# Hybrid decoder block on one core: bias parts split on ACT and DVE inside the merge, an eleventh weight tile in flight, the first gather done block by block

## Chip, cores and metric

One core of a Trainium2 chip runs the whole program. The metric is the device time of one execution in microseconds (us): median of 3 runs of the kernel before 1238.84 us (1238.54 to 1238.99). All data are float32; DMA is moved by 16 engines, and the weights of 32 experts (384 MiB) pass through the core once.

## The reference, cut to what matters

```python
h = rms_norm(x, g_norm_mix) * (1 + scale1) + shift1        # x is 256 tokens x 1024
z = h @ w_in                                               # four mixers' inputs and the merge logits
ys = ...                                                   # MoBA, GLA, retention, sliding window
up = einsum('bsnc,ncd->bsnd', ys, w_branch)
mixed = sum(sigmoid(merge_logits) * up, over the 4 branches) @ w_out
x = x + gate1 * mixed
h2 = rms_norm(x, g_norm_ffn) * (1 + scale2) + shift2
combine = softmax over the top 4 of (h2 @ w_router + b_router)   # 32 experts
for e in range(32):
    gu = h2 @ w_gate_up[e] + b_gate_up[e]                  # 1024 x 2048 weights
    act = min(glu, 7) * sigmoid(1.702 * min(glu, 7)) * (clip(lin, -7, 7) + 1)
    y += combine[:, e] * (act @ w_down[e] + b_down[e])     # 1024 x 1024 weights
out = rms_norm(x + gate2 * y, g_final)
```

## The kernel before

**Front.** Everything up to the router is one pass over the input weights. Each weight block is split into a rounded part and a remainder (function `split`, L347 on ACT writes the part `wh`, L348 on DVE the remainder `wl`), and TensorE multiplies both. The merge is the last piece of it: four branches (`for bi, n in enumerate(order)`), four units of 256 columns in each, numbered `at` 0 to 15 here. A unit makes 48 products for the merge logits (`pz_m`, L361), a sigmoid on ACT (`msg`, L816), 12 products for the branch (`pu`, L823), and on DVE `msg<-pu,msg` (L830) and the addition into `mix` (L831). In units 1 to 11 the conditioning rows are worked off beside it: accumulations `acs` on DVE (L243, L245), and in the odd units eight transposes `pmt` (L267). Units 12 to 15 also multiply by the output weights (`pw`).

**Bias parts.** The gate and up bias of the experts (32 x 2048) is added by TensorE from three bfloat16 parts whose sum is the float32 bias. They are made once: the bias is loaded three times below each other into `bgu` (L791, DMAs of the ACT queue), and GpSimd (POOL) casts, subtracts and casts again (L794, L798, L799) into `bias_sb`. The code stands at the beginning of branch 2, but a scheduler of the language orders each engine's instructions by data and by a cost of its own, so they run earlier, in units 5 to 7.

**Expert stream.** An expert's weights are six tiles of 2048 KB (`wg` x4 for gate and up, `wd` x2 for down). SP issues the loads in order, each into one of ten slots of a cyclic list (`seq`: five of `ring`, three of `rx`, one each of `hp` and `r9`), and a load waits until the products that read the slot's last tile are done. The first ten tiles (`units`: all of experts 0 and 1 but the last two of expert 1) are loaded ahead, while the merge ends and the router runs.

**Router and first gather.** `x1_logits` and the loop over `t` make the top-4 masks and the position of each token in its expert's list. `n2h` and `n2l` hold the normalised rows, split like the weights (ACT L924, L955 and DVE L927). `gather_first` then forms `he`, the 64 rows of each of the first four experts: `pm` (0/1 matrices, L1006), 32 gather products `pg` (L1019, 8 to a block of 256 channels), and a scale and shift of each block on DVE (L1030) and ACT (L1027). After a block the function `first` may use it: `gate_up_part` (L1124) multiplies two rows of 128 channels with one `wg` tile. All of `n2l` was made before the first block, and the gather products of all blocks had been put ahead of the first gate and up products. `combine` (the routing weights) and `pwt`, `psm` (L1075, L1090) follow; then experts run in pairs.

Of the kernel before, what the change touches and what calls it, by code (L numbers as in the profile page):

```python
# [20 lines left out]
P = 128  # L21
S = 256
NT = S // P
# [19 lines left out]
def hybrid_block_kernel(ctx, tc, x, c, w_ada, b_ada, g_norm_mix, w_in, w_gla_gate, b_gla_gate, g_gla_norm,  # L43
# [5 lines left out]
    def f32(ap):  # L49
        return ap.bitcast(F32)  # L50
# [313 lines left out]
    def z_unit(tiles, c0, name, token, sw=False):  # L364
        pz = bank("z", f"pz_{name}")
        for i in range(2):
            wh, wl = split(tiles[i][:, :, c0:c0 + 256], 4, 256, f"{name}_{i}", sw)
            for j in range(2):
                z_part(pz, wh[:, 2 * j:2 * j + 2, :], wl[:, 2 * j:2 * j + 2, :], 2 * i + j, token)
                bg()  # L370
                slow_step()
        return pz
# [407 lines left out]
    for bi, n in enumerate(order):  # L780
        if bi == 2:
            finish()
            mixers.close()
            add_slots(ctx.enter_context(tc.tile_pool(name="rx", bufs=EXTRA)), EXTRA)
            lb = ctx.enter_context(tc.tile_pool(name="lb", bufs=1))
            bias_sb = lb.tile([P, D], F32, tag="bias", name="bias_sb")
            bgu, bdn = bias_sb.bitcast(BF16), bias_sb[3 * NE:, :]
            sel = lb.tile([P, NE], BF16, tag="sel", name="sel")
            bt = wtile("bgu32")
            for g in range(3):  # L790
                A.dma_start(bt[NE * g:NE * g + NE, :], b_gate_up[0])  # L791
                V.tensor_copy(sel[NE * g:NE * g + NE, :], ident[NE * g:NE * g + NE, NE * g:NE * g + NE])
            A.dma_start(bdn, b_down[0])
            G.tensor_copy(bgu[0:3 * NE, :], bt[0:3 * NE, :])  # L794
            for g0 in (1, 2):
                for g in range(g0, 3):
                    r = slice(NE * g, NE * g + NE)
                    G.tensor_tensor(bt[r, :], bt[r, :], bgu[r, :], ALU.subtract)  # L798
                    G.tensor_copy(bgu[r, :], bt[r, :])  # L799
        wb = wtile(f"wb{n}").rearrange("p (k f) -> p k f", f=1024)  # L800
        nc.sync.dma_start(wb, w_branch[0, n].rearrange("(k p) f -> p k f", p=P))
        yh, yl = ysp[n]
        for u in range(4):
# [8 lines left out]
            if at == 12:  # L812
                router_weights()
            pz = z_unit(wz, (u % 2) * 256, f"m{n}_{u}", False)
            sg = mp.tile([P, 512], F32, tag="t2", name=f"msg{n}_{u}")
            A.activation(sg, pz, AF.Sigmoid)  # L816
# [38 lines left out]
    scr = cp.tile([P, NT, D], F32, tag="xn", name="scr")  # L855
    ssq2 = cp.tile([P, NT, 4], F32, tag="ssq2", name="ssq2")
    pls = [bank("z", f"pl{t}") for t in range(NT)]
    sq_i, pl_i = {}, {}
# [9 lines left out]
    def x1_logits(t, g):  # L868
# [7 lines left out]
        if g == 1 and t == 1:  # L876
            A.activation(xt[:, 0:2], pt4[:, 0:2], AF.Copy)
            V.tensor_copy(xt[:, 2:4], pt4[:, 2:4])
        else:
            A.activation(xt, pt4, AF.Copy)  # L880
# [6 lines left out]
    for k in (KC - 2, KC - 1):  # L887
        out_split(k, 0)
    units = [wg_src(e, j) for e in range(2) for j in range(4)] + [wd_src(0, j) for j in range(2)]
    half.clear()  # L890
# [21 lines left out]
    n0 = first_n2.enter_context(tc.tile_pool(name="n0", bufs=1, side="right"))  # L912
    n2h = n0.tile([P, NT, D], F32R, tag="hi", name="n2h")
    n2l = n0.tile([P, NT, D], F32R, tag="lo", name="n2l")
    comb = epa.tile([P, NT, NE], F32, tag="comb", name="comb")
# [4 lines left out]

    def n2_first(t):
        cs = slice(0, 256)
        with tc.issue_after(sq_i[NT - 1, 1]):
            A.activation(n2h[:, t, cs], x_sb[:, t, cs], AF.Copy, scale=rss[t])  # L924

    def n2_low(t, cs):
        return V.scalar_tensor_tensor(n2l[:, t, cs], x_sb[:, t, cs], rss[t], f32(n2h[:, t, cs]), ALU.mult,  # L927
                                      ALU.subtract).ins

    with tc.issue_after(pl_i[1]):  # L930
        gate_rows(5, "ab")
    for t in range(NT):
# [3 lines left out]
        rss.append(ssq2[:, t, 3:4])  # L936
        n2_first(t)
        V.scalar_tensor_tensor(lg[:, t, :], pls[t][:, 0:NE], rss[t], brt, ALU.mult, ALU.add)
# [9 lines left out]
    with tc.issue_after(mask_i):  # L948
        n2_low(0, slice(0, 256))
    V.scalar_tensor_tensor(pos, pp[:, 0:NT * NE].rearrange("p (t e) -> p t e", t=NT), 1.0, mask, ALU.add, ALU.mult)  # L950
    for q in range(1, 4):
        for t in range(NT):
            cs = slice(q * 256, (q + 1) * 256)
            with tc.issue_after(sq_i[NT - 1, 1]):
                A.activation(n2h[:, t, cs], x_sb[:, t, cs], AF.Copy, scale=rss[t])  # L955

# [25 lines left out]


    last_i = {}

# [47 lines left out]
    def gather_first(then):  # L1033
        pm, he = one_hot(0)
        with tc.issue_after(last_i["pm"]):
            n2_low(1, slice(0, 256))
        for q in range(1, 4):
            with tc.issue_after(last_i["pm"]):
                for t in range(NT):
                    n2_low(t, slice(q * 256, (q + 1) * 256))  # L1040
        for k2 in range(KC // 2):
            cs = slice(k2 * 256, (k2 + 1) * 256)
            gather_part(0, k2, pm, he, n2h[:, :, cs], n2l[:, :, cs])
            then(k2, he)
        return he, pm
# [442 lines left out]
```

## Time and profile before

| | |
|---|---|
| median of 3 runs | 1238.84 us |
| profiled execution: time / span | 1239.36 us / 1237.6 us |
| busy PE / DVE / ACT / POOL | 1137.6 / 499.1 / 236.0 / 41.6 us |
| moved by DMA | 470.40 MB, mean 380 GB/s |
| mean granted TensorE clock | 0.979 |

The span is cut into 40 slices of 30.9 us on the page; a digit is the busy share of a slice in tenths. Durations below come from the one profiled execution, starts are us from its span's beginning. PE is TensorE, SP the engine that issues most DMAs.

### The profile page before, as it was taken

To read this page: it belongs to the slowest core of one execution; us is meant where nothing else is said; L and a number is where in the kernel's file an instruction comes from. 1 tells how busy PE (TensorE), PEld (TensorE's weight loads), DVE (VectorE), ACT (ScalarE), POOL (GpSimd) and SP (SyncE) were. 2 spreads that over 40 slices of the span, in tenths; PEclk is the share of its full clock that TensorE was granted. 3 is DMA by queue.
4 is the path that set the end of the run, shared out by engine and by line. 5 is a ranking of instruction groups with operands and counts; after the bars stand their busy time and mean duration, and the time that the engine had idled before them with its cause. 6 is when DMAs were issued, how large, how long until landed. Compare 5 with 4: busy or idle time off the path is not lost.

```text
span 1237.6 us, 14530 instructions
## 1 busy us (share of the span) xinstructions
PE 1137.6 (92%) x6134; PEld 580.3 (47%) x6134; DVE 499.1 (40%) x845; ACT 236.0 (19%) x409; POOL 41.6 (3%) x64
## 2 busy tenths in 40 slices
PE   6999986999999999999989998999999898889895
PEld 4788886998433333333333333333333333333334
DVE  3597699866322323232223223222222322232244
ACT  3466332444200200020011002001100200020000
POOL 2000107000000000000000000000000000000000
PEclk9999998999999998999999999999999999999998
DMA  9977479738799999999999999999999999999994
GB/s 320 349 276 256 153 268 347 282 155 371 308 430 426 429 427 427 428 427 429 427 428 429 426 428 427 428 426 428 427 427 429 426 427 428 428 427 428 428 423 152
DMA packets 63643, 470.40 MB, mean 380 GB/s; under 512 B 6362, under 2 KB 18771, under 8 KB 39156
## 3 DMA queue, kind: packets, MB, share of 16 engines
q1 hardware_dynamic: 62736, 467.37, 91.6%
q10 hardware_dynamic: 836, 2.04, 0.5%
q8 instruction: 50, 0.82, 0.3%
q14 instruction: 21, 0.17, 0.0%
HBM read 468.35 MB, written 1.05 MB: 379 GB/s over the span
## 4 chain that ended last, share of the span: by engine, by line
PE 72%; DMA 16%; DVE 9%; issue 1%; ACT 1%; POOL 0%; POOLq 0%; ACTq 0%; DVEq 0%; SPq 0%
PE ea L1124 15%; PE ed L1150 14%; PE eb L1124 14%; DMA wg<-in_w_gate_up_dram 9%; PE pz_m L361 6%; DMA wd<-in_w_down_dram 6%; PE pg L1019 3%; PE pw L768 2%; PE py L1167 2%; DVE wl_m L348 1%; PE pu L823 1%; PE eat L1138 1%; DVE y_sb L1172 1%; DVE nl L1055 1%; DMA wada<-in_w_ada_dram 1%
## 5 line engine op out<-in xcount | busy, mean ns | idle before, releaser
L1124 PE MATMUL ea<-wg,he 128*64 128x512 f32 x1024 | 281.3, 607 | 5.0 <-DMA wg<-in_w_gate_up_dram 5.0
L1124 PE MATMUL eb<-wg,he 128*64 128x512 f32 x1024 | 278.2, 600 | 0.0
L1150 PE MATMUL ed<-wd,aT 128*64 128x512 f32 x960 | 221.4, 606 | 6.6 <-DMA wd<-in_w_down_dram 6.6
L1124 PEld LDWEIGHTS eb<-wg,he 128*64 128x64 f32 x1024 | 78.2, 139 | 149.4 <-issue 149.4
L1124 PEld LDWEIGHTS ea<-wg,he 128*64 128x64 f32 x1024 | 73.3, 138 | 129.4 <-issue 114.5
L1150 PEld LDWEIGHTS ed<-wd,aT 128*64 128x64 f32 x960 | 67.1, 139 | 133.0 <-issue 120.5
L1100 ACT ACTIVATE es<-eg 128x512 f32<-128x512 f32 x32 | 20.2, 631 | 511.2 <-DVE eg L1098 511.2
L1098 DVE TENSOR_SCALAR eg<-ea 128x512 f32<-128x512 f32 x32 | 22.1, 692 | 235.5 <-PE ea L1124 235.5
L361 PE MATMUL pz_m<-hhl,wh_m 128*128 128x256 f32 x512 | 96.9, 289 | 0.6 <-ACT wh_m L347 0.6
L361 PE MATMUL pz_m<-hhl,wl_m 128*128 128x256 f32 x256 | 73.9, 289 | 10.7 <-DVE wl_m L348 10.7
L361 PEld LDWEIGHTS pz_m<-hhl,wh_m 128*128 128x128 f32 x512 | 81.4, 195 | 1.5 <-ACT wh_m L347 0.8
L1140 DVE COPY aT<-eat 128x512 f32<-128x512 f32 x32 | 22.1, 692 | 84.0 <-PE eat L1138 84.0
L361 PEld LDWEIGHTS pz_m<-hhl,wl_m 128*128 128x128 f32 x256 | 49.9, 195 | 11.7 <-DVE wl_m L348 11.7
L1172 DVE TENSOR_TENSOR y_sb<-y_sb,py 128x512 f32<-128x512 f32 x56 | 36.0, 684 | 37.8 <-PE py L1167 37.8
L1019 PE MATMUL pg<-pm,nl 128*128 128x256 f32 x112 | 36.7, 344 | 15.7 <-DVE nl L1055 15.4
L1019 PE MATMUL pg<-pm,nh 128*128 128x256 f32 x112 | 34.6, 316 | 17.1 <-ACT nh L1054 17.1
L1160 DVE TENSOR_TENSOR obl<-ed,obh 64x512 fp32r<-64x512 f32 x30 | 20.7, 689 | 71.7 <-ACT obh L1159 71.4
L1030 DVE TENSOR_SCALAR he<-pg,G,modT 128x256 f32<-128x256 f32 x32 | 17.2, 542 | 78.9 <-PE pg L1019 78.9
L348 DVE TENSOR_TENSOR wl_m<-win_m,wh_m 128x1024 fp32r<-128x1024 f32 x26 | 44.7, 1732 | 7.6 <-ACT wh_m L347 7.6
L1054 ACT ACTIVATE nh<-x_sb,ssq 128x256 fp32r<-128x256 f32 x56 | 25.3, 499 | 80.3 <-PE pg L1019 80.3
L347 ACT ACTIVATE wh_m<-win_m 128x1024 fp32r<-128x1024 f32 x26 | 27.5, 1059 | 66.1 <-PE pz_m L361 51.4
L1019 PEld LDWEIGHTS pg<-pm,nh 128*128 128x128 f32 x112 | 21.9, 195 | 33.1 <-ACT nh L1054 27.5
(441 smaller groups left out, 1363.9 us busy)
## 6 DMA issues: line engine op xcount, KB each, us to landing
wg<-in_w_gate_up_dram SPq DMA_DIRECT2D x128, 2048.0 KB, 27.6
wd<-in_w_down_dram SPq DMA_DIRECT2D x62, 2048.0 KB, 28.8
wada<-in_w_ada_dram SPq DMA_DIRECT2D x14, 1024.0 KB, 11.3
win_m<-in_w_in_dram SPq DMA_DIRECT2D x13, 1024.0 KB, 8.8
win_c<-in_w_in_dram SPq DMA_DIRECT2D x8, 1024.0 KB
wada<-in_w_ada_dram SPq DMA_DIRECT2D x12, 512.0 KB, 7.5
wada<-in_w_in_dram SPq DMA_DIRECT2D x3, 1024.0 KB, 10.5
wo<-in_w_out_dram SPq DMA_DIRECT2D x3, 1024.0 KB, 8.3
```

The lines of the kernel that those rows point to most:

```text
L347: A.activation(wh, src, AF.Copy)
L348: V.tensor_tensor(wl, src, f32(wh), ALU.subtract)
L361: T.matmul(pz[:, b * 256:(b + 1) * 256], l, r, start=(kh == 0 and b == 0 and kk == 0 and i == 0), stop=last and i == 2, skip_group_check=True)
L768: T.matmul(pw[t, hf_], m_[:, kk, t * P:(t + 1) * P], w[:, 0, :], start=(k == 0 and i == 0), stop=(k == KC - 1 and i == 2))
L1019: last_i["pg"] = T.matmul(pg[:, kk * 256:(kk + 1) * 256], n2[:, t, :].rearrange("p (c r) -> p r c", r=2)[:, kk, :], pm[:, t, :, 0:2], star ...
L1054: A.activation(nh[:, t, :], x_sb[:, t, cs], AF.Copy, scale=rss[t])
L1098: V.tensor_scalar(g, pa, 7.0, None, ALU.min)
L1124: last_i["gu"] = T.matmul(pp_[64 * j:64 * j + 64, :], he[:, k, (e % EB) * CAP:(e % EB + 1) * CAP], w[:, i * DE + j * 512:i * DE + (j + 1) ...
L1140: V.tensor_copy(aT, pt.rearrange("p (q s) -> p q s", q=4))
L1150: last_i["ed"] = T.matmul(pd[64 * jj:64 * jj + 64, :], aT[:, k % 4, 64 * (k // 4):64 * (k // 4) + 64], w[k % 4][:, (jj ^ sw) * 512:(jj ^ s ...
L1167: T.matmul(py, s_[:, hf_, t * P:(t + 1) * P], o_, start=(i == 0), stop=(i == 1))
L1172: V.tensor_tensor(yv, yv, py, ALU.add)
```

## The change

Three edits. (1) The bias parts are made in four column pieces of 512, by `bias_part(u)` in the four units of branch 2: ACT makes the bfloat16 copies (12, over 96, 64 and 32 partitions), DVE the two subtractions of each piece (8); POOL makes none. (2) An eleventh tile is loaded ahead. The ten slots now take three `wg` tiles of expert 0, four of expert 1 and three `wd` tiles; the fourth `wg` tile of expert 0 goes into pool `n0`, where `n2h` and `n2l` lay and where the experts' work tiles lie later. (3) `n2` is kept as four blocks of 256 channels for the high and low part, the low parts are made one block at a time, and each block's gate and up products are put behind the next block's gather.

```diff
-            G.tensor_copy(bgu[0:3 * NE, :], bt[0:3 * NE, :])
-            for g0 in (1, 2):
-                for g in range(g0, 3):
-                    r = slice(NE * g, NE * g + NE)
-                    G.tensor_tensor(bt[r, :], bt[r, :], bgu[r, :], ALU.subtract)
-                    G.tensor_copy(bgu[r, :], bt[r, :])
+            def bias_part(i):
+                cs = slice(i * 512, (i + 1) * 512)
+                for g in (3, 2, 1):
+                    b, f = bgu[0:NE * g, cs], bt[0:NE * g, cs]
+                    A.activation(b, f, AF.Copy)
+                    if g > 1:
+                        V.tensor_tensor(f, f, b, ALU.subtract)
...
             pz = z_unit(wz, (u % 2) * 256, f"m{n}_{u}", False)
+            if bi == 2:
+                bias_part(u)
...
-    units = [wg_src(e, j) for e in range(2) for j in range(4)] + [wd_src(0, j) for j in range(2)]
+    units = [wg_src(0, j) for j in range(3)] + [wg_src(1, j) for j in range(4)]
+    units += [wd_src(e, j) for e in range(2) for j in range(2)][0:3]
...
-    n2h = n0.tile([P, NT, D], F32R, tag="hi", name="n2h")
-    n2l = n0.tile([P, NT, D], F32R, tag="lo", name="n2l")
+    u = wg_src(0, 3)
+    pref[u[0]] = load_wide(*u, pool=n0)
+    n2 = [[(n0 if q else epa).tile([P, NT, 256], F32R, tag=f"{tg}{q or ''}", name=f"{tg}0_{q}") for q in range(4)]
+          for tg in ("nh", "nl")]
...
-        with tc.issue_after(last_i["pm"]):
-            n2_low(1, slice(0, 256))
-        for q in range(1, 4):
-            with tc.issue_after(last_i["pm"]):
-                for t in range(NT):
-                    n2_low(t, slice(q * 256, (q + 1) * 256))
-        for k2 in range(KC // 2):
-            cs = slice(k2 * 256, (k2 + 1) * 256)
-            gather_part(0, k2, pm, he, n2h[:, :, cs], n2l[:, :, cs])
-            then(k2, he)
+        for q in range(KC // 2 + 1):
+            if 0 < q < KC // 2:
+                with tc.issue_after(last_i["pm" if q == 1 else "he"]):
+                    for t in range(NT):
+                        n2_low(t, q)
+            if q < KC // 2:
+                with tc.issue_after(last_i["gu"]) if q > 1 else nullcontext():
+                    gather_part(0, q, pm, he, n2[0][q], n2[1][q])
+            if q > 0:
+                with tc.issue_after(last_i["pg"]):
+                    then(q - 1, he)
```

**Where instructions move.** First DVE, in units 5 and 6 of the merge (`wl_m_2_0` is the remainder of the first half of unit 6, `msg_1` belongs to unit 5, `bgu<-bgu,bias_sb` is a subtraction of the bias). Before:

```order
L348 TENSOR_TENSOR wl_m_2_1_2146<-win_m_20_2113,wh_m_2_1_2145 128x1024
L830 TENSOR_TENSOR msg_1_2092<-pu_1_2098,msg_1_2092 128x512
L348 TENSOR_TENSOR wl_b_2_2176<-wada_0_1_1849,wh_b_2_2175 128x512
L831 TENSOR_TENSOR mix<-mix,msg_1_2092 128x512
L348 TENSOR_TENSOR wl_m_3_0_2216<-win_m_20_2113,wh_m_3_0_2215 128x1024
L348 TENSOR_TENSOR wl_m_3_1_2246<-win_m_20_2113,wh_m_3_1_2245 128x1024
L830 TENSOR_TENSOR msg_2_2173<-pu_2_2179,msg_2_2173 128x512
```

Now:

```order
L802 TENSOR_TENSOR bgu_2305<-bgu_2305,bias_sb 96x512 x3
L835 TENSOR_TENSOR msg_1_2092<-pu_1_2098,msg_1_2092 128x512
L348 TENSOR_TENSOR wl_m_2_1_2146<-win_m_20_2113,wh_m_2_1_2145 128x1024
L836 TENSOR_TENSOR mix<-mix,msg_1_2092 128x512
L348 TENSOR_TENSOR wl_b_2_2176<-wada_0_1_1849,wh_b_2_2175 128x512
L802 TENSOR_TENSOR bgu_2305<-bgu_2305,bias_sb 64x512 x2
L348 TENSOR_TENSOR wl_m_3_0_2216<-win_m_20_2113,wh_m_3_0_2215 128x1024
L802 TENSOR_TENSOR bgu_2305<-bgu_2305,bias_sb 64x512
L802 TENSOR_TENSOR bgu_2305<-bgu_2305,bias_sb 96x512
L348 TENSOR_TENSOR wl_m_3_1_2246<-win_m_20_2113,wh_m_3_1_2245 128x1024
L835 TENSOR_TENSOR msg_2_2173<-pu_2_2179,msg_2_2173 128x512
```

Seven of the eight subtractions stand in these two units, ahead of remainders that TensorE needs; the eighth stands in unit 8.

Second TensorE, behind the gather products of the first two blocks (`ea_3296`/`ea_3318` and `eb` are expert 0's sums, `ea_3438`/`ea_3459` expert 1's; the digit behind `wg` is the tile). Before, after 30 of the 32 gather products:

```order
L1124 MATMUL eb_3297<-wg_2_3137,he_3307 64x512 x2
L1019 MATMUL pg_3_3372<-pm_3302,n2h 128x256
L1019 MATMUL pg_3_3372<-pm_3302,n2l 128x256
L1115 LDWEIGHTS sel
...
L1124 MATMUL ea_3438<-wg_0_3141,he_3307 64x512
L1124 MATMUL ea_3296<-wg_3_3139,he_3307 64x512 x2
...
L1075 MATMUL pwt_3406<-comb_3253,pm_3302 128x4 x8
L1090 MATMUL psm_0_3432<-ident,pm_3302 128x128 x4
```

Now, after 16 gather products and the first tile's products:

```order
L1132 MATMUL eb_3319<-wg_0_3146,he_3329 64x512 x2
L1026 MATMUL pg_2_3364<-pm_3324,nh_2_3267 128x256
...
L1132 MATMUL ea_3318<-wg_1_3148,he_3329 64x512 x2
...
L1083 MATMUL pwt_3427<-comb_3274,pm_3324 128x4 x8
L1098 MATMUL psm_0_3453<-ident,pm_3324 128x128 x4
...
L1132 MATMUL ea_3459<-wg_1_3154,he_3329 64x512 x2
L1132 MATMUL eb_3460<-wg_1_3154,he_3329 64x512
L1132 MATMUL ea_3318<-wg_3_3263,he_3329 64x512 x2
```

The first tile's products stand 14 gather products earlier than before, and the products of expert 0's fourth tile now stand inside those of expert 1's second tile.

Third the load queue of SP, from the ninth load on. Before:

```order
L134 DMA wd_0_3149<-in_w_down_dram 128x4096
L134 DMA wd_1_3242<-in_w_down_dram 128x4096
L134 DMA wd_0_3524<-in_w_down_dram 128x4096
L134 DMA wd_1_3534<-in_w_down_dram 128x4096
L134 DMA wg_0_3561<-in_w_gate_up_dram 128x4096
```

Now:

```order
L134 DMA wd_1_3162<-in_w_down_dram 128x4096
L134 DMA wd_0_3255<-in_w_down_dram 128x4096
L134 DMA wg_3_3263<-in_w_gate_up_dram 128x4096
L134 DMA wd_1_3553<-in_w_down_dram 128x4096
L134 DMA wg_0_3580<-in_w_gate_up_dram 128x4096
```

The fourth `wg` tile of expert 0 is the eleventh load; `wd_1_3553` is the first load that waits for a slot to come free.

## Rows read from the trace of the kernel before

**Rows 1.** The page, section 2, the span in 40 slices.
```profile
DMA  9977479738799999999999999999999999999994
GB/s 320 349 276 256 153 268 347 282 155 371 308 430 426 429 427 427 428 427 429 427 428 429 426 428 427 428 426 428 427 427 429 426 427 428 428 427 428 428 423 152
```

**Rows 2.** Windows: length, busy us (x instructions) of PE, PEld, DVE, ACT, POOL, then PEclk, DMA share, GB/s.
```profile
190.00:220.00 30.00, 21.79 (x147) 21.09 (x148) 29.68 (x22) 6.25 (x8) 17.61 (x6) 0.83 0.94 353
220.00:260.00 40.00, 40.00 (x341) 39.84 (x340) 29.39 (x39) 16.88 (x22) 0.00 (x0) 1.00 0.66 250
...
312.00:320.00 8.00, 8.00 (x51) 4.89 (x52) 3.71 (x9) 1.48 (x3) 0.10 (x1) 1.00 0.05 19
320.00:321.00 1.00, 1.00 (x6) 0.29 (x4) 0.00 (x0) 0.00 (x0) 0.00 (x0) 1.00 1.14 229
...
400.00:600.00 200.00, 189.30 (x840) 70.42 (x837) 57.13 (x97) 23.72 (x44) 0.60 (x2) 0.97 1.01 427
```

**Rows 3.** Timeline of POOL in the merge: start, us, engine, line, operation.
```profile
184.03 1.97 POOL L794 CAST bias_sb<-bgu 96x2048 bf16<-96x2048 f32 x1 [28.52 <-DMA bgu<-in_b_gate_up_dram]
...
205.19 2.77 POOL L799 CAST bias_sb<-bgu 32x2048 bf16<-32x2048 f32 x1
```

**Rows 4.** Timeline of DVE, units 5 to 7 of the merge.
```profile
184.16 2.38 DVE L348 TENSOR_TENSOR wl_b<-wada,wh_b 128x512 fp32r<-128x512 f32 x1
186.46 10.15 DVE L348 TENSOR_TENSOR wl_m<-win_m,wh_m 128x1024 fp32r<-128x1024 f32 x2
196.53 0.68 DVE L830 TENSOR_TENSOR msg<-pu,msg 128x512 f32<-128x512 f32 x1
197.14 1.77 DVE L348 TENSOR_TENSOR wl_b<-wada,wh_b 128x512 fp32r<-128x512 f32 x1
198.83 2.37 DVE L831 TENSOR_TENSOR mix<-mix,msg 128x512 f32<-128x512 f32 x1
201.13 7.91 DVE L348 TENSOR_TENSOR wl_m<-win_m,wh_m 128x1024 fp32r<-128x1024 f32 x2
```

**Rows 5.** Groups by line, DVE, window 210 to 245 us: busy us, mean ns.
```profile
L348 DVE TENSOR_TENSOR wl_m<-win_m,wh_m 128x1024 fp32r<-128x1024 f32 x8 | 9.7, 1220 | 2.9 <-ACT wh_m L347 2.9
...
L348 DVE TENSOR_TENSOR wl_b<-bgu,wh_b 128x512 fp32r<-128x512 f32 x4 | 2.7, 684 | 0.0
```

**Rows 6.** Timeline of ACT: the sigmoids that end the logits of units 5, 7, 9, 10, 11.
```profile
188.53 0.58 ACT L816 ACTIVATE msg<-pz_m 128x512 f32<-128x512 f32 x1
...
217.27 0.58 ACT L816 ACTIVATE msg<-pz_m 128x512 f32<-128x512 f32 x1
...
231.45 0.58 ACT L816 ACTIVATE msg<-pz_m 128x512 f32<-128x512 f32 x1
...
238.46 0.58 ACT L816 ACTIVATE msg<-pz_m 128x512 f32<-128x512 f32 x1
...
246.64 0.58 ACT L816 ACTIVATE msg<-pz_m 128x512 f32<-128x512 f32 x1
```

**Rows 7.** Chain that ended last, 300 to 350 us: start, us, what.
```profile
305.97 0.88 PE pl L883 x4
...
311.44 4.01 PE pg L1019 x30
...
316.46 0.86 PE eb L1124 x4
...
326.35 0.34 PE ea L1115 x2
326.68 0.22 PE eb L1115 x2
...
331.19 0.98 PE pwt L1075 x8
332.17 0.51 PE psm L1090 x4
```

**Rows 8.** Timeline of SP from 318 us: start, us, loads issued.
```profile
319.08 3.76 SPq L134 DMA_DIRECT2D wd<-in_w_down_dram  x2
```

## Prediction before the run

> **What bounds the kernel now.** I read the slices first, then windows, then single engines at the two places that the change touches. The slices [rows 1] show two regimes. From slice 13 on the DMA digit is 9 and the rate stands at 426 to 430 GB/s until the last slice; a window of 200 us in the middle gives 427 GB/s at a share of 1.01 [rows 2]. The expert stream is bound by DMA: its end is its beginning, plus bytes over rate, plus the time in which DMA stood still. The first twelve slices are ragged, so there something else sets the pace. A microsecond there is a microsecond at the end, since the stream begins when the front releases buffers.
>
> In the front, compare two windows of the merge [rows 2]. From 220 to 260 us TensorE is busy 40.00 of 40 us. From 190 to 220 us it has 21.79 of 30, its granted clock is 0.83 (part of the stretch at the lower level, 1.2 GHz, after TensorE had stood still), and DVE is busy 29.68 of 30. DVE sets the pace there, but not by its amount of work: two remainders `wl_m` took 10.15 us and two more 7.91 [rows 4], while the same instruction takes 1.22 later [rows 5]. All of the long ones lie between 184.03 and 207.96 us, which is when POOL makes the bias parts [rows 3]. The product `msg<-pu,msg`, which reads one operand from PSUM, kept its 0.68 in the midst of it [rows 4]. So I take the POOL instructions to stretch those of DVE that read two operands from SBUF.
>
> At the seam between front and stream, DMA idles: from 312 to 320 us its share is 0.05, and of the microsecond after that a little over half was used [rows 2]. That is 8 x 0.95 + 0.5 = 8.1 us. All ten slots were full, and the first one came free with the first load at 319.08 [rows 8].
>
> **The bias parts.** The change removes every POOL instruction of that stretch. The excess on DVE, by rows 4 against 0.68 (128x512) and 1.22 (128x1024) [rows 5], is 1.70 + 7.71 + 1.09 + 1.69 + 5.47 = 17.7 us. It adds eight subtractions of 512 columns. Their price is the spacing of two such instructions, 197.14 - 196.53 = 0.61 [rows 4], so 4.9 us, which is paid on DVE, the engine that leads here: 12.8 us are left. Seen from TensorE: a unit takes 238.46 - 231.45 = 7.0 us when nothing holds it, and 8.2 with the transposes `pmt` (unit 11, 246.64 - 238.46). Unit 7 has them too, so from 188.53 the logits of unit 7 could end at 188.53 + 7.0 + 8.2 = 203.7 instead of 217.27 [rows 6], a gain of 13.6. I take **13.0**, between the two views, and nearer to DVE's. The lower bound is 6: the subtractions stand ahead of remainders that TensorE waits for, and three of the chain's steps change engine in every piece. The upper bound is 15.3: the 13.6, and the 1.7 by which unit 5's own `wl_b` was long [rows 4].
>
> The twelve copies go to ACT, busy 6.25 of 30 us there [rows 2]; at the 0.58 of a sigmoid of the same width [rows 6] they cost 7 us of its idle time. Behind them on ACT stand `wh` of unit 6 and later ones; those also wait for TensorE to give back their buffers, and that covers them. If the cover goes, they lengthen a unit by a copy. The first copy waits for the bias from DRAM, landed at 184.03 [rows 3], about when ACT gets to it. I cost that at nothing.
>
> The trace says that DVE's 29.68 us are mostly blocking. The Trainium skill, in Perfetto Trace Analysis, section Optimizing Scalar/DVE Operations, advises moving work off a saturated DVE to ScalarE or even GPSIMD, which speaks against this edit, though it warns in the same place of a port that the two share. By the first half of that rule the edit would cost 4.9 us instead of gaining 13.0.
>
> Does the earlier front meet another limit? DMA is busy at 353 GB/s from 190 to 220 us [rows 2], so its loads run ahead. From 220 to 260 it needs only 0.66 of its time, so I let it cover the shift. All later releases, the expert prefetch and the router then move by the same 13.0.
>
> **The eleventh tile.** 2048 KB at 427 GB/s are 4.9 us. Its room was the front's, whose last readers are the router's products, done at 306.85 [rows 7]; the queue runs dry at 312.4, so the tile is queued in time and DMA goes on to 317.3 (clock of before). The Trainium skill, in SBUF — State Buffer, section A bandwidth-pool intuition that's wrong, gives about 358 GB/s from HBM to a core. A tile would be 5.9 us by that, an estimate, and the sum 1 us lower. The window's 427 decides here.
>
> **The first gather.** Thirty products took 4.01 us [rows 7], so the sixteen now ahead take 2.1. With 0.2 for the end of `he` the first tile starts at 313.8. Four rows of 0.86 [rows 7] make a tile's sixteen multiplications 3.4 us, so the slot is free at 317.2 instead of 319.1. From issue to first bytes it takes 1.3 us (319.08 to about 320.4 [rows 2, 8]), so DMA idles from 317.3 to 318.5, 1.2 us. Four further loads carry it to 318.5 + 4 x 4.9 = 338.1. The fifth needs the second tile of expert 1. Ahead of its release TensorE now has 2 x 1.1 of gather, 2 x 3.4 of tiles, 0.56 of bias, 1.49 of `pwt` and `psm` [rows 7], 3.4 + 3.4 of tiles of expert 1 and, put between, 3.4 of expert 0's fourth: 317.2 + 21.3 = 338.5, with the delay 339.8. DMA stands still once more, 1.7 us. The sum is 8.1 - 1.2 - 1.7 = 5.2; I take **5.0**. The block order's 1.9 us are thus lent and given back, and the tile's 4.9 are what stays. The bounds are 4.0 (fifth release a microsecond later) and 6.9 (never waited for). The low parts, made one block at a time, lie on DVE while TensorE multiplies; I cost them at nothing.
>
> **The sum.** The profiled execution took 1239.36 us; less 13.0 and 5.0 it is 1221.4. The median of the runs is 0.52 lower, so I give **1220.8**.
>
> **The rivals.**
> 1. *Only the front gains.* The eleventh load waits longer for its room, or the later releases of the ring eat it: 1225.8. For it: the fifth load already waits by my reckoning. Chance 0.09.
> 2. *Half of the front.* In units 5 to 9 DVE has its own work, 29.39 of 40 us in the following window [rows 2], and eight more subtractions in ACT's and DVE's alternation; 6 instead of 13: 1227.8. Chance 0.08.
> 3. *DVE is saturated by its own work.* The 4.9 us come on top: 1238.84 + 4.9 - 5.0 = 1238.7. That is the skill's rule taken alone. Against it stand the durations in rows 4 beside rows 5. Chance 0.03.
> 4. *Slower: the long DVE instructions come from the DMA writes.* DMA was full in that stretch as well; then the long ones stay and the subtractions are stretched like `wl_b`, 8 x 2.38 = 19.0 [rows 4]: 1238.84 + 19.0 - 5.0 = 1252.8. It turns slower once a subtraction costs over 0.63 us with no excess gone. Against it: `msg` kept its 0.68 among the long ones. Chance 0.03.
> 5. *Both parts at their best*, 15.3 + 6.9: 1216.6. Chance 0.05.
>
> **How the numbers follow.** My forecast has 0.72; its own range is 1217.4 to 1223.8. For 8 in 10 I give 1217 to 1227, which takes in the forecast and rival 1 and leaves out the others. A measurement of this kernel tells 0.2%, 2.5 us, from no change. Faster: 0.72 + 0.09 + 0.08 + 0.05 = 0.94; same: 0.03; slower: 0.03.
>
> **What would show it.** In the changed profile: no POOL work between 180 and 210 us; `wl_m` in units 6 and 7 at 1.2 us; the sigmoid of unit 7 at about 204; DMA still for about 3 us instead of 8 around the first gather, in two pieces; the expert stream at 427 GB/s. `wl_m` still at 5 us would overturn the first term, a still time of 8 us the second, and a rate under 420 GB/s in the stream both.

## The result and the profile after

The changed kernel takes 1224.68 us in the median of 4 runs (1222.81 to 1225.99) against 1238.69 for the kernel before (4 runs, 1237.92 to 1238.99): ratio 0.9887, 95% interval 0.9870 to 0.9904, or 14.0 us less. 1220.8 was forecast, 1217 to 1227 as the range. The profiled execution is the fastest of the four (1222.81 us, span 1221.1, mean granted clock 0.989; the other three 0.981 or 0.982), so its gain of 16.55 us on the profiled execution of before is more than the median's.

The page's slices of the change, to be held against [rows 1]: DMA's busy tenths and GB/s.

```profile
DMA  9976479939999999999999999999999999999993
GB/s 316 352 290 241 173 250 388 358 128 426 381 430 427 428 429 427 427 428 427 426 428 428 427 427 429 427 428 427 427 427 428 427 427 428 428 427 427 428 422 140
```

The stream runs at 426 to 430 GB/s as before; the hollow ahead of it (128 GB/s, 155 before) stays, and two slices on 381 instead of 308 is the seam, where the standstill was. Windows of the change (width, PE, PEld, DVE, ACT, POOL busy, granted clock, DMA share, GB/s), to be held against [rows 2]:

```profile
190.00:200.00 10.00, 10.00 (x86) 9.90 (x85) 10.00 (x15) 7.85 (x14) 0.00 (x0) 1.00 1.04 397
200.00:210.00 10.00, 10.00 (x86) 9.99 (x85) 10.00 (x13) 4.19 (x5) 0.00 (x0) 1.00 1.05 395
210.00:220.00 10.00, 9.70 (x82) 9.50 (x81) 10.00 (x12) 5.70 (x8) 0.00 (x0) 1.00 1.04 396
280.00:320.00 40.00, 39.11 (x227) 24.25 (x227) 19.34 (x55) 12.50 (x28) 1.88 (x4) 1.00 1.00 422
320.00:324.00 4.00, 4.00 (x20) 1.29 (x18) 1.42 (x3) 0.66 (x1) 0.00 (x0) 1.00 0.95 324
324.00:328.00 4.00, 3.90 (x20) 1.48 (x18) 2.23 (x4) 1.25 (x2) 0.00 (x0) 1.00 0.87 336
328.00:332.00 4.00, 4.00 (x22) 1.38 (x20) 0.38 (x1) 0.00 (x0) 0.00 (x0) 1.00 1.02 385
332.00:336.00 4.00, 4.00 (x20) 1.20 (x16) 2.73 (x4) 0.63 (x1) 0.00 (x0) 1.00 0.91 344
```

From 190 to 220 us TensorE is busy nearly throughout (21.79 of 30 before) at the full clock, POOL does nothing ([rows 3] have no answer), and DVE is full. DMA goes on without a standstill until 320, then runs low for 16 us: (103 + 91 + 42 + 83) x 4 / 427 = 3.0 us lost.

DVE in unit 5 and 6 of the merge, against [rows 4], and the sigmoids of units 7, 10 and 15 on ACT, against [rows 6]:

```profile
185.47 1.23 DVE L348 TENSOR_TENSOR wl_m<-win_m,wh_m 128x1024 fp32r<-128x1024 f32 x1 [0.56 <-ACT wh_m L347]
...
190.48 1.22 DVE L348 TENSOR_TENSOR wl_m<-win_m,wh_m 128x1024 fp32r<-128x1024 f32 x1
...
192.81 1.28 DVE L802 TENSOR_TENSOR bgu<-bgu,bias_sb 64x512 f32<-64x512 f32 x2
194.02 1.21 DVE L348 TENSOR_TENSOR wl_m<-win_m,wh_m 128x1024 fp32r<-128x1024 f32 x1
```

```profile
204.37 0.58 ACT L821 ACTIVATE msg<-pz_m 128x512 f32<-128x512 f32 x1
...
226.28 0.58 ACT L821 ACTIVATE msg<-pz_m 128x512 f32<-128x512 f32 x1
...
275.64 0.58 ACT L821 ACTIVATE msg<-pz_m 128x512 f32<-128x512 f32 x1
```

Every `wl_m` has its 1.2 us back, a subtraction costs 0.6, and unit 7's sigmoid stands at 204.37 instead of 217.27, a lead of 12.90 us; by unit 10 it is 12.18, and that goes on to unit 15 (287.82 before). The router on TensorE, in the place of the first rows of [rows 7]:

```profile
292.77 1.09 PE L889 MATMUL pl<-wr,scr 128*128 128x32 f32 x8
293.69 2.03 PE L296 MATMUL pb<-ident,modT 128*128 128x128 f32 x16
295.56 0.18 PE L958 MATMUL ppos<-mask,ustr 128*128 128x32 bf16 x1
...
296.62 0.36 PE L1026 MATMUL pg<-pm,nh 128*128 128x256 f32 x1 [0.34 <-DVE pm L1013]
```

The first `pg` comes 296.62 - 275.64 = 20.98 us behind the sigmoid of unit 15. Before it was 311.37 - 287.82 = 23.55: there the clock was at its lower level (granted 0.50) from 305 to 312 us, and `pb`, 16 products that nobody reads, took 3.76 us ahead of the last `ppos`. In the trace of before:

```profile
287.82 0.58 ACT L816 ACTIVATE msg<-pz_m 128x512 f32<-128x512 f32 x1
...
306.66 3.76 PE L296 MATMUL pb<-ident,modT 128*128 128x128 f32 x16
```

This 2.57 us is no term of the forecast. Last, SP's issues of the first, fourth and fifth load into a freed slot, against [rows 8]:

```profile
302.41 0.33 SPq L134 DMA_DIRECT2D wd<-in_w_down_dram  x1
...
318.26 0.33 SPq L134 DMA_DIRECT2D wg<-in_w_gate_up_dram  x1
...
325.13 0.33 SPq L134 DMA_DIRECT2D wg<-in_w_gate_up_dram  x1
```

The fourth is issued 15.9 us behind the first, where three loads of 4.9 us take 14.7, and the fifth 22.7 us behind it, where four take 19.6: that is where DMA runs short.

### The profile page after: what moved, and what is told of

It is laid out like the page before. It is cut to its first block, busy times and chain, and to the rows that moved or that the text cites. A ratio compares the mean times of both kernels' runs of the same rounds, so it can differ in the third digit from the quotient of the medians.

```text
span 1221.1 us, 14530 instructions
## 1 busy us (share of the span) xinstructions
PE 1126.1 (92%) x6134; PEld 572.8 (47%) x6134; DVE 486.2 (40%) x853; ACT 242.3 (20%) x421; POOL 18.0 (1%) x57
## 4 chain that ended last, share of the span: by engine, by line
PE 59%; DMA 16%; DVE 8%; issue 1%; ACT 0%; POOL 0%; POOLq 0%; DVEq 0%; SPq 0%; ACTq 0%
PE ea L1132 14%; PE ed L1158 14%; PE eb L1132 14%; DMA wg<-in_w_gate_up_dram 10%; DMA wd<-in_w_down_dram 6%; PE pg L1026 3%; PE pz_m L361 3%; PE pw L768 2%; PE py L1175 2%; DVE y_sb L1180 1%; PE eat L1146 1%; DVE nl L1063 1%; DVE he L1037 1%; PE psm L1098 1%; PE pu L828 1%
## 5 line engine op out<-in xcount | busy, mean ns | idle before, releaser
L1026 PE MATMUL pg<-pm,nl 128*128 128x256 f32 x128 | 40.7, 336 | 15.8 <-DVE nl L1063 15.8
L1026 PE MATMUL pg<-pm,nh 128*128 128x256 f32 x128 | 38.9, 316 | 17.4 <-ACT nh L1062 17.1
L1026 PEld LDWEIGHTS pg<-pm,nh 128*128 128x128 f32 x128 | 25.2, 197 | 35.6 <-ACT nh L1062 27.5
L1026 PEld LDWEIGHTS pg<-pm,nl 128*128 128x128 f32 x128 | 25.1, 197 | 28.7 <-DVE nl L1063 21.3
L1167 ACT ACTIVATE oah<-ed 64x512 fp32r<-64x512 f32 x30 | 17.7, 592 | 100.4 <-PE ed L1158 89.2
```

What stands on the lines that cost most here:

```text
L1026: last_i["pg"] = T.matmul(pg[:, kk * 256:(kk + 1) * 256], n2[:, t, :].rearrange("p (c r) -> p r c", r=2)[:, kk, :], pm[:, t, :, 0:2], star ...
```

## The experiments

Runs of one kernel spread by 1 to 7 us, as much as the smaller effects. The kernels were timed in five batches, each beside the kernel before (medians 1238.1 to 1238.8 us), so a difference of under 1 us between batches is not read. Each trace is also measured by stages. **u15 - u3** is the time from the sigmoid of unit 3 to that of unit 15, **pg - u15** from there to the first gather product, **1st** and **5th** the issue of the first and fifth load into a freed slot, and **140 MB** the moment when DMA has moved that much (GB/s summed over windows of 5 us), the last three counted from the first `pg`. From 140 to 450 MB all fourteen traces take 724.9 to 725.1 us: behind the seam they are alike.

| kernel | median (runs), us | u15 - u3 | pg - u15 | 1st | 5th | 140 MB |
|---|---|---|---|---|---|---|
| before | 1238.69 | 117.34† | 23.55* | 7.71 | 24.9 | 133.3 |
| after | 1224.68 (1222.8 to 1226.0) | 105.52* | 20.98 | 5.79 | 28.5 | 130.7 |
| e1 bias only | 1225.42 (1224.2 to 1227.5) | 105.69* | 23.65* | 7.55 | 24.8 | 133.0 |
| e2 tile and order | 1235.21 (1231.2 to 1238.3) | 117.75*† | 21.01 | 5.78 | 28.5 | 130.3 |
| e3 no tile | 1226.11 (1224.9 to 1226.6) | 105.77* | 22.63* | 5.79 | 24.2 | 132.7 |
| e4 no order | 1223.32 (1222.3 to 1225.7) | 105.70* | 23.56* | 7.16 | 28.2 | 130.0 |
| e5 half fill | 1225.00 (1224.7 to 1226.5) | 104.28 | 22.93* | 7.69 | 30.4 | 132.7 |
| e6 hold | 1222.07 (1221.3 to 1222.5) | 105.54* | 23.57* | 5.84 | 22.6 | 127.8 |
| e7 POOL casts | 1228.27 (1224.9 to 1230.4) | 108.25† | 20.99 | 5.79 | 28.5 | 130.3 |
| e8 POOL subtractions | 1223.27 (1221.8 to 1225.5) | 106.80† | 20.99 | 5.78 | 28.5 | 130.2 |
| e9 hold, split fill | 1219.38 (1217.3 to 1221.4) | 105.63* | 21.26 | 5.79 | 22.6 | 127.7 |
| e10 hold, no order | 1220.12 (1217.4 to 1222.9) | 104.24 | 23.49* | 7.38 | 22.5 | 127.9 |
| e11 hold, POOL subtractions | 1221.04 (1219.1 to 1223.9) | 105.70 | 21.00 | 5.78 | 22.6 | 127.7 |
| e12 POOL in pieces | 1231.77 (1229.6 to 1235.7) | 111.80† | 21.04 | 7.47 | 24.7 | 132.9 |

A star marks a stretch in which the clock fell to its lower level, in the merge at 172 to 178 us, in the router between 290 and 312. A dagger marks a fall later in the merge, between 192 and 215 us, where TensorE stood still for 1.8 to 5.6 us; all five are kernels with work on POOL.

### The parts alone: e1 to e4

**e1**, the kernel before with the bias edit only: `bias_part` in the place of the POOL lines, its call behind `z_unit`.

> The kernel before with the bias parts alone split on ACT and DVE; ten tiles, gather as before. Theory: the long DVE instructions came from the POOL instructions beside them, and the merge carries its 12.2 us (measured at the logits of unit 10 in the trace of the change) to the end: 1238.7 - 12.2 = 1226.5 us; DMA stands still about as long as before (8.1 us) ahead of the first freed load, 5 us if TensorE's clock does not fall in the router. Rival, the gain is taken back at the first gather because the ten slots are then full sooner: a still time of 8 + 12 us and a time near 1238. Rival, the change's gain of 14 to 16 us is all in this part: 1224 us or less.

Measured: 1225.42 us, ratio 0.9893 (0.9878 to 0.9907), 13.2 us less. The merge has all of the change's lead (105.69 against 105.52) and loses nothing of it later; the seam behind the first `pg` is that of before (133.0 against 133.3). Theory held: 1226.5 was expected, and the interval is 1223.5 to 1227.1 us. Of the rivals the first (1238) is excluded by the time, the second (all of the gain in this part) by the seam alone.

**e2**, the change with the six POOL lines of before.

> The changed kernel with the bias parts made on POOL in one piece again; eleventh tile and block order stay. Theory: units 5 to 7 take as long as before (wl_m above 5 us beside POOL, logits of unit 10 at 238.5 us), and what is left is the seam's share, 4 to 5 us: 1238.7 - 4.5 = 1234.2 us. Rival, the seam's part needs the earlier merge and gives nothing alone: 1238.7 us. Rival, the router's clock fall goes away through the new order and adds 2.6 us: 1231.6 us.

Measured: 1235.21 us, ratio 0.9978 (0.9966 to 0.9991), 3.4 us less. Units 5 to 7 are long again, the seam is that of the change. Tile and order by themselves thus gave 1.1 to 4.2 us: the theory's 1234.2 lies at the edge of the interval (1234.4 to 1237.5), both rivals outside. Its profiled execution had no fall of the clock in the router; its twelve runs lie between 1231.2 and 1238.3 us.

**e3**, the change without the eleventh tile:

```diff
-    units = [wg_src(0, j) for j in range(3)] + [wg_src(1, j) for j in range(4)]
-    units += [wd_src(e, j) for e in range(2) for j in range(2)][0:3]
+    units = [wg_src(e, j) for e in range(2) for j in range(4)] + [wd_src(0, j) for j in range(2)]
...
-    u = wg_src(0, 3)
-    pref[u[0]] = load_wide(*u, pool=n0)
```

> The changed kernel without the eleventh tile: the fourth tile of expert 0 lies in the ten slots again, bias parts and block order stay. Theory of the prediction (the tile's 4.9 us stay, the block order is lent and given back): 1224.7 + 4.9 = 1229.6 us. Second theory, that in the change the release of the second tile of expert 1 caps what the tile gives: the first freed load comes as early as in the change (302.4 us), DMA stands still ahead of it for some 3 to 6 us and no longer at the fifth, so only 2 to 3.5 us are lost: 1227 to 1228 us. Rival, the tile does nothing: 1224.7 us.

Measured: 1226.11 us (ratio 0.9901, 0.9886 to 0.9915), 1.4 more than the change, which the two intervals don't separate. The 4.9 us of the forecast are excluded; the median lies under the second theory's 1227 to 1228, and its trace (132.7 against 130.7) gives the tile 2.0 us.

**e4**, the change with all low parts and (but for five products) all gather products first:

```diff
-        for q in range(KC // 2 + 1):
...
+        for q in range(1, KC // 2):
+            with tc.issue_after(last_i["pm"]):
+                for t in range(NT):
+                    n2_low(t, q)
+        for q in range(KC // 2):
+            gather_part(0, q, pm, he, n2[0][q], n2[1][q])
+            then(q, he)
```

> The changed kernel without the block order: all low parts first, the gather products of all blocks ahead of the first gate and up products, bias parts and eleventh tile stay. Theory, that the release of the second tile of expert 1 sets the end of the seam: the first freed load comes about 2 us later than in the change, the fifth at the same time, and the time is that of the change within 0.7 us: 1224.7 us. Rival, the block order carries its own 1.9 us: 1226.6 us.

Measured: 1223.32 us (ratio 0.9876, 0.9862 to 0.9891), no slower than the change. The first freed load is 1.4 us later (7.16), the fifth is not (28.2 against 28.5). So the block order is worth nothing: by the last column it takes 0.3 us off without the tile (e3 against e1) and adds 0.7 with it (the change against e4). The tile alone is worth 3.0 (e4 against e1), not 4.9.

### What caps the seam: e6 and e10

**e6** puts the products of expert 0's fourth tile, the eleventh loaded, behind those of three tiles of expert 1. By this `pwt` and `psm` move behind them too: they stand 29.4 us behind the first `pg` in its trace, 16.5 in the change's.

```diff
-    he, pm = gather_first(first)
-    first_n2.close()
+    he, pm = gather_first(lambda q, h: first(q, h) if q < 3 else None)
     g0_i = last_i["pg"], last_i["pg"]
+    gate_up(1, he, range(6))
+    with tc.issue_after(last_i["gu"]):
+        first(3, he)
+    first_n2.close()
...
```

> The changed kernel with the products of expert 0's fourth tile (the eleventh tile loaded) put behind those of the first three tiles of expert 1. Theory, that TensorE, busy without a pause from the first gather on, reaches the end of the second tile of expert 1 28.5 us after the first gather product and that this release (the fifth freed load) is what keeps DMA waiting 3 us in the change: now it comes 22 to 23 us after it, DMA stays at 420 to 430 GB/s from 300 to 350 us, and the time falls by 2.5 to 3.5 us to about 1221.7 us. Rival, the loads that follow (expert 0's down tiles, released later now) wait instead and take it back: 1224 to 1226 us. Rival, the low rate from 320 to 336 us comes from something else: 1224.7 us.

Measured: 1222.07 us, ratio 0.9865 (0.9848 to 0.9881), 2.6 less than the change, and all four runs within 1.2 us. Its windows:

```profile
304.00:308.00 4.00, 4.00 (x24) 1.89 (x22) 1.33 (x3) 0.56 (x1) 0.00 (x0) 1.00 0.70 221
...
312.00:316.00 4.00, 4.00 (x22) 1.38 (x20) 1.46 (x8) 1.68 (x3) 0.00 (x0) 1.00 0.94 373
316.00:320.00 4.00, 4.00 (x22) 1.33 (x20) 0.00 (x0) 0.00 (x0) 0.00 (x0) 1.00 0.96 332
320.00:328.00 8.00, 8.00 (x40) 2.69 (x38) 0.00 (x0) 0.00 (x0) 0.00 (x0) 1.00 1.00 426
328.00:332.00 4.00, 4.00 (x26) 2.05 (x24) 2.90 (x7) 1.92 (x2) 0.00 (x0) 1.00 1.03 442
```

The low rate from 320 to 336 us is gone, and the later releases do not take it back. Shown: TensorE's work ahead of the late releases capped the change. The fifth, of expert 1's second tile, comes 22.6 instead of 28.5 us behind `pg`, and the fourth, of its first tile, 19.2 instead of 21.6; what each of the two is worth, and what of it `pwt` and `psm` gave, is not separated. What is left, 3.3 us from 304 to 320, lies at the first loads, in an execution whose clock had fallen in the router.

**e10** takes the block order away from e6.

> The kernel with the held fourth tile, without the block order (the gather of all blocks ahead of the first gate and up products). Theory: once the release of expert 1's second tile no longer caps the seam, the first freed load does, and the block order, which brings it 1.9 us forward, is worth that: 1222.1 + 1.9 = 1224 us, with the first freed load issued 7.6 us behind the first gather product instead of 5.8. Rival, TensorE's later releases still decide and the order is worth nothing: 1222.1 us or less.

Measured: 1220.12 us (ratio 0.9855, 0.9835 to 0.9875): the theory fell. The first freed load does come 1.5 us later, and yet 140 MB come at 127.9, as in e6 with 127.8. The windows say why:

```profile
300.00:304.00 4.00, 4.00 (x22) 1.55 (x22) 0.63 (x2) 1.25 (x3) 0.00 (x0) 1.00 0.59 250
304.00:308.00 4.00, 4.00 (x20) 1.29 (x18) 0.00 (x0) 0.00 (x0) 0.00 (x0) 1.00 0.74 242
308.00:312.00 4.00, 4.00 (x23) 1.67 (x21) 0.31 (x1) 0.00 (x0) 0.00 (x0) 1.00 1.00 430
312.00:316.00 4.00, 4.00 (x22) 1.36 (x20) 2.09 (x11) 2.10 (x3) 0.00 (x0) 1.00 1.00 426
```

It loses (177 + 185) x 4 / 427 = 3.4 us at once and nothing after, e6 loses 1.9 first and 1.4 at 312 to 320. Both reach the fourth release at the same distance (315.68 - 296.65 = 19.0, 318.45 - 299.25 = 19.2): the work ahead of it is the same in either order. The median is 2 us lower than e6's. Of the 3.2 us between the two profiled executions 1.2 lie ahead of unit 3 and 1.3 in the merge, which ran here without a fall of the clock; that the order costs anything is not shown.

### TensorE's clock in the router: e5 and e9

**e5** is the change with half of `pb` (`gate_rows(5, "a")` for `"ab"`).

> The changed kernel with 8 instead of 16 of the products pb, whose result nobody reads and which stand on TensorE between the router's logits and the last product ppos. In the traces of the first four runs these 16 took 3.6 to 3.8 us where TensorE's clock fell to its lower level (granted 0.50) and 2.03 us where it did not, and ppos, the masks ready, waited behind them. Theory, that this wait is the 2.6 us between pg of the change (21.0 us behind the sigmoid of unit 15) and pg of the runs with a fallen clock (22.6 to 23.7 us): with 8 the wait is gone even at the lower level, pg comes 21 to 22 us behind that sigmoid in any case, the median falls by 1 to 2 us to about 1223 us. Rival, the shorter fill lets the clock fall more often or longer, into the gather's products: 1225 to 1228 us.

Measured: 1225.00 us (ratio 0.9895, 0.9878 to 0.9911), nothing gained. First its rows in the router, then those of e4, whose `pb` is whole; in both the clock had fallen.

```profile
293.64 2.05 PE L296 MATMUL pb<-ident,modT 128*128 128x128 f32 x8
...
296.62 0.21 PE L958 MATMUL ppos<-mask,ustr 128*128 128x32 bf16 x1
297.70 0.55 PE L1026 MATMUL pg<-pm,nh 128*128 128x256 f32 x1 [0.87 <-DVE pm L1013]
```

```profile
295.78 3.76 PE L296 MATMUL pb<-ident,modT 128*128 128x128 f32 x16
299.34 0.23 PE L958 MATMUL ppos<-mask,ustr 128*128 128x32 bf16 x1
```

`ppos` waits less in e5 (pg - u15 is 22.93 against 23.56), but then TensorE pauses, the clock stays low until 302 us, and the gather runs at it: the first slot is free 7.69 us behind `pg` instead of 5.79. So the rival's mechanism is what the trace shows, and the wait on `pb` alone isn't the price: a fallen clock is.

**e9** is e6 with `gate_rows(5, "a")` behind `pl_i[0]` and `"b"` behind `pl_i[1]`.

> The kernel with the held fourth tile, and half of the products pb moved forward into the pauses of the router's logits on TensorE (behind the first token block's logits instead of all behind the second's). In e6 the clock fell in the router in the profiled run, and the mean clock of its four runs (0.981 to 0.983) says that it fell in all. Theory, that the fall comes after the pauses and small products of the logits: with TensorE fed there the clock stays at 1.00 from 285 to 300 us, pg comes 21 to 21.7 us behind the sigmoid of unit 15 instead of 23.6, and the time falls by 1 to 2.5 us from 1222.1 us. Rival, the fall comes by itself in some executions and not in others: nothing gained, 0.5 us lost to the products in front of the logits: 1222 to 1223 us.

Measured: 1219.38 us, ratio 0.9849 (0.9834 to 0.9864), the lowest median, though its interval overlaps those of e6, e10 and e11: 2.7 less than e6 (2.0 by the ratios), 5.3 less than the change. Its windows in the router:

```profile
288.00:292.00 4.00, 3.79 (x32) 3.59 (x32) 2.38 (x8) 2.11 (x5) 0.13 (x1) 1.00 1.03 440
292.00:296.00 4.00, 3.76 (x33) 3.07 (x32) 3.00 (x14) 2.74 (x7) 0.56 (x1) 1.00 0.97 412
296.00:300.00 4.00, 3.19 (x22) 2.48 (x24) 3.35 (x10) 1.63 (x4) 0.76 (x2) 1.00 1.03 434
```

The clock stays at 1.00, pg - u15 is 21.26 instead of 23.57, and the mean clock of its five runs is 0.985 to 0.990 where e6 had 0.981 to 0.983. That fits the theory. It isn't proof: in after, e2, e7, e8, e11 and e12 the profiled execution kept its clock with the old fill too.

### Which work on POOL costs what: e7, e8, e11, e12

**e7** makes the copies with `G.tensor_copy`, **e8** the subtractions with `G.tensor_tensor`; **e11** is e8 with the hold of e6.

> The changed kernel with the twelve copies of the bias parts on POOL instead of ACT; the subtractions stay on DVE. Theory, that any POOL instruction on SBUF stretches those instructions of DVE beside it that read two operands from SBUF: wl_m beside a cast takes 2 to 5 us instead of 1.2; with some 7 to 10 us of POOL work and the 0.75 us of excess for each us of POOL that the kernel before shows (17.7 over 23.7 us), 5 to 7 us are lost: 1230 to 1232 us. Rival, only POOL's two-operand subtractions do that: wl_m keeps 1.2 us, 1224.7 us or 1 us more where a subtraction on DVE waits for a cast.

> The changed kernel with the eight subtractions of the bias parts on POOL instead of DVE; the copies stay on ACT. POOL subtractions of 32x2048 took 4.4 to 4.7 us in the kernel before, so eight of 512 columns take 9 to 10 us. Theory, that POOL stretches DVE's two-operand instructions: DVE is spared 5 us of its own subtractions and loses 0.75 x 9.5 = 7 us, which comes to 1226 to 1228 us, with wl_m at 2 to 5 us beside POOL. Rival, the stretching in the kernel before came from the DMA writes or from the long pieces alone: DVE is spared 5 us and loses nothing, 1224 us or less.

> The kernel with the held fourth tile and with the eight subtractions of the bias parts on POOL (pieces of 512 columns), the copies on ACT. In e8, against the change, the merge ended 1.6 us later (sigmoid of unit 15 at 277.3 instead of 275.6 us) but the clock did not fall in the router in its profiled run, and the mean clock of its four runs was 0.986 to 0.990. Theory, that the two are independent and e8's clock was chance: 1222.1 + 1.6 = 1223.7 us, less where the clock stays up. Rival, the later subtractions keep the clock up in most runs: 1221 us or less.

Measured: e7 1228.27 us (ratio 0.9923, 0.9904 to 0.9942), e8 1223.27 (0.9878, 0.9858 to 0.9897), e11 1221.04 (0.9868, 0.9853 to 0.9883). For e8 the time is the rival's, the trace is not. DVE and POOL of e8:

```profile
190.67 1.66 DVE L836 TENSOR_TENSOR mix<-mix,msg 128x512 f32<-128x512 f32 x1
192.25 1.65 DVE L348 TENSOR_TENSOR wl_b<-wada,wh_b 128x512 fp32r<-128x512 f32 x1
193.82 2.18 DVE L348 TENSOR_TENSOR wl_m<-win_m,wh_m 128x1024 fp32r<-128x1024 f32 x1
```

```profile
190.32 4.59 POOL L802 TENSOR_TENSOR bgu<-bgu,bias_sb 64x512 f32<-64x512 f32 x3 [1.08 <-ACT bias_sb L800]
```

Beside the three POOL subtractions of this row (1.5 us each) three DVE instructions are 0.96 us too long; with two short ones later it is 3.1 us over all eight, where DVE was spared 4.9. So both halves of the theory are there, with less excess than the 7 us expected. Still the merge is 2.5 us longer than that of e5 (106.80 against 104.28). The excess isn't the reason; a chain over three engines is. On ACT a copy waits for POOL, `wh_m` (196.01 us) stands behind the copy, DVE waits for `wh_m`, and TensorE for DVE:

```profile
194.95 1.15 ACT L800 ACTIVATE bias_sb<-bgu 32x512 bf16<-32x512 f32 x2 [0.94 <-POOL bgu L802]
197.08 1.35 DVE L348 TENSOR_TENSOR wl_m<-win_m,wh_m 128x1024 fp32r<-128x1024 f32 x1 [1.08 <-ACT wh_m L347]
199.09 0.74 PE L267 MATMUL pmt<-ident,acs 128*128 128x128 f32 x4 [1.75 <-DVE msg L835]
```

e11 has the same chain and a pause of 1.70 us there, and its merge took 105.70, 1.4 us over e5. The other 1.1 us of e8 go with the clock, which fell behind that pause in e8 (first row) and not in e11 (second):

```profile
200.00:205.00 5.00, 5.00 (x32) 5.00 (x31) 5.00 (x9) 1.52 (x2) 0.00 (x0) 0.66 1.04 395
200.00:205.00 5.00, 5.00 (x44) 4.93 (x42) 5.00 (x8) 2.68 (x4) 0.00 (x0) 1.00 1.04 398
```

That e8's median hides this by a clock that held elsewhere (mean 0.986 to 0.990 in its four runs) is likely and not shown. e11 as a whole (1221.0 us, clock 0.984 to 0.988) is 1 us under e6; neither of its theories is decided by it.

In e7, twelve casts kept POOL busy 18.1 us and cost the merge 4.0 us (108.25 against 104.28). Casts do stretch DVE's instructions, as the theory had it, but only by 2.6 us in all (`wl_m` at 1.63 and 2.18, not 2 to 5); two casts were held up themselves, to 3.41 and 4.00 us where others took 0.6 to 1.6, and TensorE stood still for 2.45 us, with a fall of the clock. The time lies between the theory's and the rival's. Its profiled execution is the fastest of its four, and the median loses 3.6 us on the change.

**e12**, the kernel before with POOL's work cut into four column pieces:

```diff
...
+            for i in range(4):
+                cs = slice(i * 512, (i + 1) * 512)
+                for g in (3, 2, 1):
+                    b, f = bgu[0:NE * g, cs], bt[0:NE * g, cs]
+                    G.tensor_copy(b, f)
+                    if g > 1:
+                        G.tensor_tensor(f, f, b, ALU.subtract)
```

> The kernel before, the bias parts all on POOL as there, but in four column pieces of 512 (20 instructions instead of 7); nothing else is changed. Theory, that an instruction of DVE with two operands in SBUF waits for the end of the POOL instruction beside it, so that its excess is that instruction's length: the excess of one falls from 3.85 us (wl_m beside subtractions of 4.6 us) to about 1 us (e8, subtractions of 1.4 us) and 0.4 us (e7, casts), over some ten such instructions 5 to 9 us instead of 17.7; the sigmoid of unit 8 comes at 213 to 217 us instead of 224.5, the time falls to 1228 to 1232 us. Rival, the excess is a share of POOL's busy time, however cut: POOL works 24 us or more, 17 us of excess stay, 1238 us or more.

Measured: 1231.77 us, ratio 0.9957 (0.9945 to 0.9968), 6.3 less than before, as the theory had it; POOL was busy 21.5 us, hardly less than before (23.5). The merge is 5.5 us shorter. The excess fell from 17.7 to 10.2 us, more than the 5 to 9 expected, and 5.9 of it is one instruction that breaks the rule of one wait; DVE first, then POOL:

```profile
191.86 3.73 DVE L348 TENSOR_TENSOR wl_m<-win_m,wh_m 128x1024 fp32r<-128x1024 f32 x2
195.51 0.68 DVE L831 TENSOR_TENSOR msg<-pu,msg 128x512 f32<-128x512 f32 x1
196.11 0.68 DVE L270 TENSOR_REDUCE ade<-pmt 128x4 f32<-128x512 f32 x1
196.71 6.62 DVE L832 TENSOR_TENSOR mix<-mix,msg 128x512 f32<-128x512 f32 x1
```

```profile
197.14 2.29 POOL L800 TENSOR_TENSOR bgu<-bgu,bias_sb 96x512 f32<-96x512 f32 x2
199.38 1.15 POOL L798 CAST bias_sb<-bgu 64x512 bf16<-64x512 f32 x2
200.51 2.27 POOL L800 TENSOR_TENSOR bgu<-bgu,bias_sb 64x512 f32<-64x512 f32 x2
202.73 1.62 POOL L798 CAST bias_sb<-bgu 32x512 bf16<-32x512 f32 x2
```

`mix` (0.69 us alone) lasted through six POOL instructions that stood back to back, and into a seventh, while `msg` and `ade`, with one operand or one from PSUM, kept their 0.68.

## Why the prediction held its range, and what was mis-sized

The profiled pair adds up by stages: 0.36 us from ahead of unit 3, 11.82 in the merge, 2.57 in the router, 2.56 in the seam, 0.8 lost at the end, behind 450 MB, for a reason left open: 16.5, which is the difference of the spans (1237.6 - 1221.1).

**Bias parts, 13.0: right.** By the medians it is 13.2 (e1). By the traces, where neither has a fallen clock at 172 to 178 us, it is 117.34 - 104.28 = 13.1 (e5), 13.1 with e10 too; the change's own trace has such a fall and shows 11.8. The falls of before at 192 and 206 us belong to the effect: TensorE had just waited 2.8 and 4.6 us for DVE. The steps hold one by one: no POOL work in the stretch, `wl_m` at 1.2 us, subtractions at 0.6, the copies free on ACT. DVE's lack of reserve fits the lead that shrinks from 12.9 at unit 7 to 12.2 at unit 10. The half of the rule in the Trainium skill (Perfetto Trace Analysis, section Optimizing Scalar/DVE Operations) by which rival 3 was made doesn't hold here: DVE, busy 29.68 of 30 us, took 4.9 us of work more and the merge became 13.1 us shorter, while e7, e8, e11 and e12, with work on POOL, have merges 1.4 to 7.5 us longer than e5's. The warning that stands beside it does.

**Eleventh tile and order, 5.0: right in kind, twice too large.** Measured from the first `pg` it is 133.3 - 130.7 = 2.6 us; e2's median gives 3.4. The step that failed is "317.2 + 21.3 = 338.5" for the fifth load with "1.7 us" of standstill: from the first freed load to the fifth it took 22.7 us, the fourth was late already, and DMA lost 3.0 us, as a rate of 324 to 385 GB/s over 16 us and not as a pause. That "the tile's 4.9 are what stays" was thus wrong although the cap had been seen; that the block order's 1.9 us "are thus lent and given back" was right (e4, e10). The pause of 1.2 us ahead of the first load was too small as well for the router's clock that the forecast had taken over from before: e6, with this order and a fallen clock, lost 1.9 us at 304 to 308. In the change's trace it didn't occur, as the clock held.

That this trace shows DMA short by about 3 us instead of 8, as the prediction had asked for, is in part luck. From 15 us ahead of the first `pg` to 40 behind it, DMA moved 360 GB/s before and 401 in the change, which against 427 is 8.6 and 3.3 us lost. But e12, with the seam of before and a clock that held in the router, moved 382 GB/s and lost 5.8: half of the fall is the clock's, not the tile's.

**Not foreseen: the clock.** The forecast took before's router as fixed. Between a held and a fallen clock lie 2.6 us in the router and 1.2 in the merge; of fourteen traces seven have the fall in the router, and seven the one at 172 to 178 us in the merge. Only one execution of a kernel has a trace, so that these falls make the whole spread of its runs is likely and not shown. With 13.1 and 2.6, and none of the clock, the forecast would have been 1238.84 - 15.7 = 1223.1; the rest to the median's 1224.7 is within its interval (1222.6 to 1226.8).

**Rivals.** DVE saturated by itself, and DMA writes as the cause, are excluded: the long instructions are gone with DMA at 395 GB/s in the same stretch. "Only the front gains", 1225.8, lies nearer to the median than the forecast does; the traces (e1 against after, 133.0 and 130.7) still give tile and order 2 to 3 us, and so does e2 against before (3.4); the medians of e1 and the change differ by only 0.7.

The stream's 427 GB/s held in every trace, so the figure of 358 in the Trainium skill (SBUF — State Buffer, section A bandwidth-pool intuition that's wrong) is not what this core alone gets.

## What to carry to other kernels

A long instruction on DVE that reads two operands from SBUF is to be held against POOL's row before it is called work; moving POOL's part away, or at least cutting it, gave most of the difference back here, and the 4.9 us that it cost DVE were cheap against 17.7. A load ahead is worth its full transfer only up to the next release that comes late: add up what the multiplying engine does until each release, and move work that frees nothing (here the extra tile's own products) behind the releases. Where runs scatter by as much as the effect, measure each trace by stages that no later stage can hide.

## What the runs showed of the hardware

DVE and POOL held each other up. Excess of one DVE instruction with two SBUF operands was 3.9 us beside POOL subtractions of 4.6, 0.96 beside those of 1.5, 0.35 to 0.96 beside casts (e7, e12), and 5.9 where at least six POOL instructions followed each other without a gap (e12). The other way round, a cast on POOL took 4.00 us in e7 where others of 512 columns took 0.6 to 1.6. The Trainium skill (SBUF — State Buffer, section Who interferes with whom) describes a lock held for a whole instruction between GpSimd and a DVE instruction with two SBUF inputs; the traces agree for both sides, and e12 adds that the wait can last over several instructions of POOL.

TensorE's clock fell to the lower level (1.2 GHz, granted 0.50) in the router in six of the twelve traces with the old fill and not in the others, after the same instructions with nearly the same pauses (0.2 us, then 0.35 to 0.47, among the small products of the logits); it came back after 3.4 to 6.8 us, and in e5, where a pause of 0.87 us followed, after 10.2. In the merge all fourteen have a pause of 2.2 us on TensorE that ends at 172 to 174 us, and in seven the clock falls there. What decides is open.

From 140 to 450 MB nothing differs: 310 MB took 725 us in fourteen kernels, within 0.3 us.
